# Seven edits to a two-layer transformer kernel: conv border, first pair behind a border, score banks, last head, last weights, constants, first norm

## The chip, the cores and the metric

The kernel runs on one core of a Trainium2 chip, as one launch. The metric is the device time of that launch in microseconds (us). The core has a matrix engine (PE), a vector engine (DVE), an activation engine (ACT) and a general one (POOL), each with its own stream of instructions; SP here only issues DMAs. PE's results go to PSUM, eight banks of 128 x 512 floats; all else lives in SBUF.

## The reference

256 tokens x and 256 context tokens ctx of 1024 features go through two layers. Both layers have the same frame; the middle part is a short convolution in layer 0 and attention (8 query heads of 128, 2 key heads) in layer 1.

```python
def _modulate(t, g, shift, scale):
    return _rms(t, g) * (1 + scale) + shift

def _swiglu(h, w13, w2):
    gte, up = jnp.split(h @ w13, 2, axis=-1)
    return (jax.nn.silu(gte) * up) @ w2
...
    mod = (jax.nn.silu(c) @ mod_w[i] + mod_b[i]).reshape(bsz, 3, 3, 1, D_MODEL)
    lat = lat + 0.5 * mod[:, 0, 2] * _swiglu(_modulate(lat, norm_g[i, 0], mod[:, 0, 0], mod[:, 0, 1]), ffn_w13[i, 0], ffn_w2[i, 0])
    h = _modulate(lat, norm_g[i, 1], mod[:, 1, 0], mod[:, 1, 1])
    y = _short_conv_mixer(h, ...) or _gqa_mixer(h, hc, ...)
    lat = lat + mod[:, 1, 2] * y
    lat = lat + 0.5 * mod[:, 2, 2] * _swiglu(_modulate(lat, norm_g[i, 2], mod[:, 2, 0], mod[:, 2, 1]), ffn_w13[i, 1], ffn_w2[i, 1])
```

The context has the same steps with modulation values of its own (modc) for as long as a later layer reads it. So there are four FFN blocks (0,0), (0,1), (1,0), (1,1), with a mixer between the two of a layer, and a root-mean-square norm over the features ahead of each of the six parts. All is in fp32.

## The kernel before, in words

**Layout.** x holds both token sets as 8 feature tiles (k or m) of 128 partitions by 512 columns, 256 tokens (s = 0) beside 256 context tokens (s = 1). Every fp32 product is three PE matmuls (mm3, L138 to L140): weights and inputs are split into a high part, rounded by an ACT cast (wh, hh, th, bh), and a low part, the rest, by a DVE subtraction (wl, hl, tl, bl); PE adds high by high, high by low, low by high. So each weight tile costs a load (SP), a cast (ACT, L114, L498, L744), a subtraction (DVE, L115, L503, L747) and then PE. Raw weights have two buffers of 2048 columns (wr, load_w L123), the split ones four of 1024 (wh, wl). Half of the FFN's gate/up tiles are done as such plain pairs, the others as block pairs (class Pair), in which sums of weights and of inputs save products: DVE makes the sums (L762 to L769) and the combinations (L804 to L820).

**Order.** In the stretches that the change touches the kernel has a manual schedule: each engine runs its instructions in the order in which the source issues them. Elsewhere a scheduler orders them. SP issues nearly all loads, in order.

**Modulation units.** Beside the first two chunks, the modulation vectors are dot products on DVE: a unit (mod_unit L152) multiplies a 128 x 1024 tile of mod_w (wm, two buffers, loaded by SP at L184) by silu(c) and adds up along the row, 128 x 1024 elements a unit. They are put between other work by tick(n) (L193), which adds n to an account and issues one unit for each whole one in it. PER_PAIR = 0.7 is what a block pair ticks.

**Borders.** Between two parts stands a norm over x that needs the last feature tiles of the part before. class Border (L397) and open_border (L530) write this out. The last two tiles (m = 6, 7) are done in halves: late(s, i) is PE's product for half s of tile 6 + i, fin(i, s) adds the result to x (DVE, L429), square and scaled are ACT's square (L437) and its product with the scale (L412), add adds the square to acc (DVE, L442), sums (PE, L256) adds up acc and the last square over the partitions, root and inv give the reciprocal root, rows (L276) spreads it. PE's order is late(0,0), late(0,1), the first mid tiles of late(1,0), sums(0), the rest of it, rows(0), late(1,1). short is the border behind the conv mixer's output projection, whose products have 8 tiles of depth (nk = KT) in place of 22. There the casts and subtractions of the four weight tiles of the next FFN's first pair (whi, wlo, L498 and L503) stand behind late(0,0), followed by tick(2), which lets DVE do two units ahead of fin(0,0). border_ffn (L825) goes on from there: it does the first gate/up tiles of the FFN in parts, so that PE starts on the tiles of x that are ready, and hands over to the loop over block pairs in ffn (L917). It is used twice, at the FFN blocks (0,1) and (1,0). Its last lines issue post[1].gl() (L906), DVE's subtraction for the second tile's result; the first pair of the loop ticks PER_PAIR at L980.

**The first norm** (L1213 on). Constants come in small loads: ccol (the vectors c), modb, normg, ident (a unit matrix), rowsum on ACT's queue, x in four quarters of two feature tiles each on SP's queue. PE runs 18 matmuls on ones (fill, L1051) in the meantime. The squares of the 8 tiles of x are done by DVE (0, 1, 7) and ACT (2 to 6), added in pairs by DVE (pair_sum, L1125), and summed over features by PE (token_sums, L1129: four matmuls a pair, 128 tokens each, one column of output). ACT's root and DVE's reciprocal follow, then PE spreads the result over the partitions (rb, L1237), and over_rms (L1173) multiplies x by it. Ahead of rb, PE does mod_pe(1, 0), behind it mod_pe(0, 0) (L1142): the first quarter of the scale and of the shift of this norm, as products of silu(c) with rows of mod_w (mr). mod_turn (L1154) turns each from a row to a column, with ACT's copy (row, L1147) ahead of it, and DVE adds bias and one (A, mod). norm_q(0) then makes hh (ACT) and hl (DVE), with which the first gate and up products start (L1202).

**Attention.** use_banks (L1724) gives PSUM to psc (scores, two tiles of two banks), ptp and pav, in that order; at that point the last q projection pq[3] is still in the first banks. weigh (L1655) multiplies the exponentials of a head, two tiles of 128 x 512, by the reciprocal sums on POOL (L1661); PE then turns them (L1672).

**The last projection** (L2013). w_last loads the weights of two output tiles at a time: two pieces of 2048 columns (w2l) and one of 12 x 128 = 1536 (w2m), all three through the two wr buffers.

Of the kernel before, what the change touches and what calls it, by code (L numbers as in the profile page):

```python
# [1 line left out]

# [27 lines left out]
PER_PAIR = 0.7  # L30
WARM = 18
FILL = 5

# [8 lines left out]
def hybrid_kernel(ctx: ExitStack, tc: tile.TileContext, a: dict, out: bass.AP):  # L42
# [29 lines left out]
    def psum(s="ps"):  # L72
        return banks["psm"].tile([P, T2], F32, tag="mm", name=nm(s))
# [3 lines left out]

    def cload(key, shape, eng=None):
        t = const.tile(list(shape), F32, name=key, tag=key)
        (eng or nc.scalar).dma_start(t, a[key])  # L80
        return t


    ccol = cload("ccol", [P, KT, 2])
    x = act.tile([P, KT, T2], F32, name="x", tag="x")
    for q in range(4):
        nc.sync.dma_start(x[:, 2 * q : 2 * q + 2, :], a["xT"][:, 2 * q : 2 * q + 2, :])
    modb = cload("modb", [P, 2, 72])
    normg = cload("normg", [P, 2, 3, KT])
    ident = cload("ident", [P, P])  # L90
    ones = const.tile([P, 1], F32, name="ones", tag="ones")
# [8 lines left out]
    nc.vector.memset(sccol, 0.0)  # L100
    rowsum = cload("rowsum", [P, 2])
    scbc = mp.tile([P, 2, D], F32, name="scbc", tag="scbc", bufs=1)
# [427 lines left out]
    def open_border(bd, v, early=False):  # L530
# [5 lines left out]
        def whi(i):  # L536
            v[i][0].hi(v[i][1])

        def wlo(i):
            v[i][0].lo(v[i][1])  # L540

        ready()
        for s in range(2):
            for k in (4, 5):
                bd.scaled(k, s)
        bd.late(0, 0)
        if short:
            for i in range(2):
                whi(i)
                wlo(i)  # L550
        tick(2)
        bd.fin(0, 0)
# [4 lines left out]
        bd.add(0)  # L557
        bd.fin(1, 0)
        bd.square(1, 0)
        bd.late(1, 0, range(mid))  # L560
# [264 lines left out]
    def border_ffn(l, b, h, bd):  # L825
# [79 lines left out]
        pr.sub(2)  # L905
        post[1].gl()  # L906
        pp.append((psum("pg"), psum("pu")))
        for s in range(2):
# [8 lines left out]
    def ffn(l, b, h, gate, norm, gs=(), ev=1.5, bd=None):  # L917
# [3 lines left out]
        for t in range(2):  # L921
            between = ()
            with tc.manual_schedule(engines=set(QUEUES[:3])) if bd else nullcontext():
# [29 lines left out]
                with nullcontext() if bd else tc.manual_schedule(engines=set(QUEUES[:3])):  # L953
                    for i in range(i1, n):
# [24 lines left out]
                        if prev:  # L979
                            tick(PER_PAIR)  # L980
                            prev.seven()
# [144 lines left out]

    def token_sums(ps, j):
        for i in range(4):
            nc.tensor.matmul(  # L1129
                ps[:, i : i + 1], sqs[2 * j][:, i * P : i * P + P], ones,  # L1130
                start=j == 0 and i == 0, stop=j == 3, skip_group_check=True,
            )
# [80 lines left out]
    with tc.manual_schedule(engines=set(QUEUES)):  # L1213
        for ch, q in ((1, 0), (0, 0)):
            ask_mod(ch, q)
        for i in range(3):
            ask_w(i, 0)
        table(AF.Silu)
        nc.scalar.activation(out=sccol[:, :, :2], in_=ccol, func=AF.Silu)
        table(AF.Sqrt)  # L1220
        nc.vector.tensor_scalar(
            out=sb1, in0=modb[:, 0, KT : 2 * KT], scalar1=1.0, scalar2=None, op0=ALU.add
        )
        ps = psum("ss")
        fill(idle, WARM)
        for k, eng in enumerate((nc.vector, nc.vector) + (nc.scalar,) * 5 + (nc.vector,)):
            square(k, eng)
            if k % 2:
                pair_sum(k // 2)
                token_sums(ps, k // 2)  # L1230
        rs = tp.tile([P, 4], F32, name="rs4", tag="rs4", bufs=1)
        nc.scalar.activation(out=rs, in_=ps[:, :4], func=AF.Sqrt, scale=1.0 / D, bias=eps_t)
        nc.vector.reciprocal(rs, rs)
        mod_pe(1, 0)
        rb = psum("rb")
# [17 lines left out]
        for ch, q in ((1, 1), (0, 1)):  # L1253
            ask_mod(ch, q)
# [51 lines left out]
    for i in range(3):  # L1306
        gs0.append(new_pair("g"))
        w13_post(pps[i], gs0[i], 0, T2)

    convk = cload("convk", [P, 3, KT], nc.sync)  # L1310
    qg = cload("qg", [P, 1], nc.sync)
    kg = cload("kg", [P, 1], nc.sync)


# [340 lines left out]
    def weigh(hd):  # L1655
        e, sm = es[hd]
        r = ap.tile([P, 2], F32, name=nm("r"), tag="r", bufs=3)
        nc.vector.reciprocal(r, sm)
        for qt in range(2):
            c = slice(qt * T2, qt * T2 + T2)  # L1660
            nc.gpsimd.tensor_scalar(  # L1661
                out=e[:, c], in0=e[:, c], scalar1=r[:, qt : qt + 1], scalar2=None, op0=ALU.mult
            )
# [35 lines left out]
    with tc.manual_schedule(engines=set(QUEUES)):  # L1699
# [313 lines left out]
    def w_last(m):  # L2013
        if m // 2 not in box:
            t = m // 2
            box[t] = (
                load_w(a["w2l"][t, 0]), load_w(a["w2l"][t, 1]), load_w(a["w2m"][t], 12 * P)
            )
        o = m % 2
        return lambda k: box[m // 2][o](k * P) if k < 16 else box[m // 2][2]((o * 6 + k - 16) * P)  # L2020

# [8 lines left out]
def _layout(inp):  # L2030
# [52 lines left out]
    d["ident"] = np.eye(P, dtype=np.float32)  # L2083
    d["rowsum"] = (np.arange(P)[:, None] % 32 == np.arange(2)).astype(np.float32)
    return {k: np.ascontiguousarray(v) for k, v in d.items()}

# [18 lines left out]
```

## Time and profile before

| | us |
|---|---|
| median of 3 runs | 1577.05 (1576.33 to 1577.66) |
| profiled execution | 1575.96 |
| its span, first to last instruction | 1573.9 |
| PE busy | 1557.0 |
| DVE busy | 1286.5 |
| ACT busy | 755.2 |
| POOL busy | 34.2 |
| mean granted clock of PE | 0.996 |

How to read it: the profile's page has each engine's busy time, the chain of work that ended last, the costliest groups of instructions and the DMA queues. The trace behind it answers narrower questions: what an engine waited for (a row of the list of waits has the waiting instruction, what released it, us in total, times, longest), when instructions ran (a row of the timeline has start, duration, engine, line, operation, and in brackets the idle time ahead of it with its releaser), and a table by windows of time (for each engine the busy us and, in brackets, the instructions; then the clock that PE was granted, the DMA engines' busy share and GB/s).

### The profile page before, as it was taken

To read this page: it belongs to the slowest core of one execution; us is meant where nothing else is said; L and a number is where in the kernel's file an instruction comes from. 1 tells how busy PE (TensorE), PEld (TensorE's weight loads), DVE (VectorE), ACT (ScalarE), POOL (GpSimd) and SP (SyncE) were. 2 spreads that over 40 slices of the span, in tenths; PEclk is the share of its full clock that TensorE was granted. 3 is DMA by queue.
4 is the path that set the end of the run, shared out by engine and by line. 5 is a ranking of instruction groups with operands and counts; after the bars stand their busy time and mean duration, and the time that the engine had idled before them with its cause. 6 is when DMAs were issued, how large, how long until landed. Compare 5 with 4: busy or idle time off the path is not lost.

```text
span 1573.9 us, 25256 instructions
## 1 busy us (share of the span) xinstructions
PE 1557.0 (99%) x10240; PEld 1422.7 (90%) x10240; DVE 1286.5 (82%) x1905; ACT 755.2 (48%) x1261; POOL 34.2 (2%) x28
## 2 busy tenths in 40 slices
PE   9999999999999989999999999999999999999998
PEld 7789899989888889998999899988999899998887
DVE  5788879996999578996999878997998776776654
ACT  4524245535322365532554475532554465775542
POOL 0000000000000000000000000000000002320000
PEclk9999999999999999999999999999999999999999
DMA  9363633363566412355334523357335632345553
GB/s 360 131 209 130 205 111 131 105 212 132 196 214 199 136 67 99 130 188 162 120 122 146 202 95 121 126 197 240 125 131 194 211 124 87 108 161 193 192 176 136
DMA packets 51747, 248.75 MB, mean 158 GB/s; under 512 B 6704, under 2 KB 9264, under 8 KB 36400
## 3 DMA queue, kind: packets, MB, share of 16 engines
q1 hardware_dynamic: 50912, 246.98, 46.1%
q8 instruction: 80, 1.31, 0.3%
q14 instruction: 35, 0.29, 0.1%
q10 hardware_dynamic: 720, 0.17, 0.0%
HBM read 244.77 MB, written 1.05 MB: 156 GB/s over the span
## 4 chain that ended last, share of the span: by engine, by line
PE 94%; DVE 2%; ACT 1%; DMA 1%; issue 0%; POOL 0%; ACTq 0%; DVEq 0%; POOLq 0%
PE py L138 9%; PE py L140 9%; PE py L139 9%; PE p L138 6%; PE p L140 6%; PE p L139 6%; PE q L140 5%; PE q L138 4%; PE q L139 4%; PE pu L1817 3%; PE pg L1817 3%; PE py L1817 2%; PE pg L522 2%; PE pu L522 2%; PE pg L1202 1%; PE pv L138 1%
## 5 line engine op out<-in xcount | busy, mean ns | idle before, releaser
L114 ACT ACTIVATE wh<-wr 128x1024 fp32r<-128x1024 f32 (+1 forms) x210 | 190.7, 926 | 248.4 <-PE py L139 128.1
L157 DVE CUSTOM_DVE_ANT_0 junk<-wm,scbc,modb 128x1024 bf16<-128x1024 f32 x224 | 286.9, 1281 | 24.6 <-DMA wm<-in_modT 22.7
L115 DVE TENSOR_TENSOR wl<-wr,wh 128x1024 fp32r<-128x1024 f32 (+1 forms) x210 | 220.1, 1060 | 71.8 <-ACT wh L114 29.7
L138 PE MATMUL py<-gh,wh 128*128 128x512 f32 (+1 forms) x594 | 217.8, 367 | 0.0
L139 PE MATMUL py<-gl,wh 128*128 128x512 f32 (+1 forms) x594 | 217.3, 366 | 0.0
L140 PE MATMUL py<-gh,wl 128*128 128x512 f32 (+1 forms) x594 | 217.1, 365 | 0.0
L747 DVE TENSOR_TENSOR wl<-wr,wh 128x1024 fp32r<-128x1024 f32 x156 | 186.1, 1218 | 27.7 <-ACT wh L744 27.7
L744 ACT ACTIVATE wh<-wr 128x1024 fp32r<-128x1024 f32 x156 | 160.5, 1056 | 100.5 <-DVE wr L767 59.0
L140 PEld LDWEIGHTS py<-gh,wl 128*128 128x128 f32 x594 | 112.1, 189 | 17.9
L138 PEld LDWEIGHTS py<-gh,wh 128*128 128x128 f32 x594 | 112.1, 189 | 17.7
L139 PEld LDWEIGHTS py<-gl,wh 128*128 128x128 f32 x594 | 112.1, 189 | 17.6
L140 PE MATMUL p<-th,wl 128*128 128x256 f32 x416 | 117.7, 283 | 0.0
L139 PE MATMUL p<-tl,wh 128*128 128x256 f32 x416 | 117.7, 283 | 0.0
L138 PE MATMUL p<-th,wh 128*128 128x256 f32 x416 | 117.7, 283 | 0.0
L138 PE MATMUL q<-bh,wh 128*128 128x256 f32 x304 | 86.0, 283 | 0.0
L139 PE MATMUL q<-bl,wh 128*128 128x256 f32 x304 | 86.0, 283 | 0.0
L140 PE MATMUL q<-bh,wl 128*128 128x256 f32 x304 | 86.0, 283 | 0.0
L139 PEld LDWEIGHTS p<-tl,wh 128*128 128x128 f32 x416 | 79.8, 192 | 0.2
L138 PEld LDWEIGHTS p<-th,wh 128*128 128x128 f32 x416 | 79.8, 192 | 0.2
L140 PEld LDWEIGHTS p<-th,wl 128*128 128x128 f32 x416 | 79.8, 192 | 0.0
L762 DVE TENSOR_TENSOR wr<-wr 128x1024 f32<-128x1024 f32 x52 | 63.7, 1225 | 1.6
L114 ACT ACTIVATE gh<-gm 128x512 fp32r<-128x512 f32 x60 | 37.8, 631 | 52.1 <-DVE gm L820 47.7
(372 smaller groups left out, 4098.1 us busy)
## 6 DMA issues: line engine op xcount, KB each, us to landing
wr<-in_w SPq DMA_DIRECT2D x85, 1024.0 KB, 4.8
wm<-in_modT SPq DMA_DIRECT2D x128, 512.0 KB, 4.2
wr<-in_w2h SPq DMA_DIRECT2D x48, 704.0 KB, 5.3
mr<-in_mod SPq DMA_DIRECT2D x16, 512.0 KB, 8.5
wr<-in_cw_cx SPq DMA_DIRECT2D x8, 1024.0 KB, 4.8
wr<-in_w2l SPq DMA_DIRECT2D x8, 1024.0 KB, 4.9
wr<-in_cw_b SPq DMA_DIRECT2D x4, 1024.0 KB, 5.2
wr<-in_cw_out SPq DMA_DIRECT2D x4, 1024.0 KB, 5.7
```

What stands on the lines that cost most here:

```text
L114: nc.scalar.activation(out=hi, in_=src, func=AF.Copy)
L115: nc.vector.tensor_tensor(out=lo, in0=src, in1=hi.bitcast(F32), op=ALU.subtract)
L138: nc.tensor.matmul(ps, wh, mh, start=first, stop=False, **kw)
L139: nc.tensor.matmul(ps, wh, ml, start=False, stop=False, **kw)
L140: nc.tensor.matmul(ps, wl, mh, start=False, stop=last, **kw)
L157: nc.vector.tensor_tensor_reduce(out=junk, in0=raw, in1=scbc[:, v, :], scale=1.0, scalar=modb[:, l, col : col + 1], op0=ALU.mult, op1=ALU.add,
L522: nc.tensor.matmul(ps, w[n == 1], hl if n == 2 else hh, start=first and n == 0 and k == ks[0] and (first is True or g == 0), stop=last and ...
L744: nc.scalar.activation(out=self.shaped(g, 0), in_=self.part(g), func=AF.Copy)
L747: nc.vector.tensor_tensor(out=self.shaped(g, 1), in0=self.part(g), in1=self.shaped(g, 0).bitcast(F32), op=ALU.subtract,)
L762: tt(out=by_two(raw[:, :1024]), in0=a21.unsqueeze(1).to_broadcast([P, 2, T2]), in1=by_two(raw)[:, :, :T2], op=ALU.subtract,)
L1202: nc.tensor.matmul(pps[i][j], w[j][n == 1], hl if n == 2 else hh, start=k == 0 and n == 0, stop=k == KT - 1 and n == 2,)
L1817: nc.tensor.matmul(p[:, :n], w(j, k)[part], m(k)[:, :n], start=not part and k == 0, stop=part == 1 and k == nk - 1, skip_group_check=True,)
```

## The change

- **Conv border** (open_border, short alone): the casts and subtractions of the next FFN's first weights are issued ahead of ready(), so ahead of late(0,0) and of the scaled tiles; tick(2) ahead of fin(0,0) becomes tick(1), and a tick(1) stands behind fin(1,0).
- **First pair behind a border**: tick(2) behind post[1].gl(); the first pair of the loop ticks 0 in place of 0.7.
- **Scores**: the banks are given out in the order ptp, pav, psc, so the scores' tiles are in the last four banks.
- **Eighth head**: weigh(7) runs on DVE, the others stay on POOL.
- **Last projection**: w2m comes in two pieces of 768 columns, one for each output tile, through the modulation rows' buffers (wm).
- **Constants**: all eight come in one load of 128 x 364 floats on ACT's queue (convk, qg, kg with them, which SP loaded behind the first norm's loads).
- **x**: the fourth quarter is issued by ACT, the others by SP.
- **First norm**: squares on DVE for 0, 2, 4, on ACT for the others; token sums over pair 0, pair 2, tile 6 alone, pair 4, tile 7 alone; four fills ahead of rb in place of mod_pe(1, 0); behind over_rms the order is product and turn of the scale, product and turn of the shift, with the first weights' casts and subtractions ahead of and behind the last turn; the copy of rb comes behind norm_q(0).

```diff
+CONSTS = (
+    ("ccol", (KT, 2)), ("modb", (2, 72)), ("normg", (2, 3, KT)), ("ident", (P,)),
+    ("rowsum", (2,)), ("convk", (3, KT)), ("qg", (1,)), ("kg", (1,)),
+)
...
+    cst = const.tile([P, sum(sizes)], F32, name="cst", tag="cst")
+    nc.scalar.dma_start(cst, a["cst"])
...
     for q in range(4):
-        nc.sync.dma_start(x[:, 2 * q : 2 * q + 2, :], a["xT"][:, 2 * q : 2 * q + 2, :])
+        eng = nc.scalar if q == 3 else nc.sync
+        eng.dma_start(x[:, 2 * q : 2 * q + 2, :], a["xT"][:, 2 * q : 2 * q + 2, :])
...
+        if short:
+            for i in range(2):
+                whi(i)
+                wlo(i)
         ready()
         for s in range(2):
             for k in (4, 5):
                 bd.scaled(k, s)
         bd.late(0, 0)
-        if short:
-            for i in range(2):
-                whi(i)
-                wlo(i)
-        tick(2)
+        tick(1 if short else 2)
         bd.fin(0, 0)
...
         bd.fin(1, 0)
+        if short:
+            tick(1)
         bd.square(1, 0)
...
         post[1].gl()
+        tick(2)
         pp.append((psum("pg"), psum("pu")))
...
-                            tick(PER_PAIR)
+                            tick(0 if bd and i == i1 else PER_PAIR)
...
-    def token_sums(ps, j):
+    def token_sums(ps, k):
         for i in range(4):
             nc.tensor.matmul(
-                ps[:, i : i + 1], sqs[2 * j][:, i * P : i * P + P], ones,
-                start=j == 0 and i == 0, stop=j == 3, skip_group_check=True,
+                ps[:, i : i + 1], sqs[k][:, i * P : i * P + P], ones,
+                start=k == 0 and i == 0, stop=k == 7, skip_group_check=True,
             )
...
+        ps = psum("ss")
+        fill(idle, WARM)
+        square(0, nc.vector)
+        square(1, nc.scalar)
+        square(2, nc.vector)
+        pair_sum(0)
+        token_sums(ps, 0)
+        square(3, nc.scalar)
+        square(4, nc.vector)
+        pair_sum(1)
+        token_sums(ps, 2)
+        square(5, nc.scalar)
+        square(6, nc.scalar)
+        token_sums(ps, 6)
+        pair_sum(2)
+        token_sums(ps, 4)
+        square(7, nc.scalar)
+        token_sums(ps, 7)
         nc.vector.tensor_scalar(
             out=sb1, in0=modb[:, 0, KT : 2 * KT], scalar1=1.0, scalar2=None, op0=ALU.add
         )
...
-        mod_pe(1, 0)
+        fill(idle, 4)
         rb = psum("rb")
...
         over_rms(0, rb)
-        ris = tp.tile([P, T2], F32, name="ris", tag="gm", bufs=3)
-        nc.scalar.copy(ris, rb)
+        mod_pe(1, 0)
+        mod_turn(1, 0)
         mod_pe(0, 0)
         w_hi(0, 0)
+        mod_turn(0, 0)
         w_lo(0, 0)
-        mod_turn(1, 0)
-        mod_turn(0, 0)
...
         norm_q(0)
+        ris = tp.tile([P, T2], F32, name="ris", tag="gm", bufs=3)
+        nc.scalar.copy(ris, rb)
...
-            nc.gpsimd.tensor_scalar(
+            eng = nc.vector if hd == HEADS - 1 else nc.gpsimd
+            eng.tensor_scalar(
                 out=e[:, c], in0=e[:, c], scalar1=r[:, qt : qt + 1], scalar2=None, op0=ALU.mult
             )
...
-        use_banks(("psc", 2), ("ptp", 2), ("pav", 2))
+        use_banks(("ptp", 2), ("pav", 2), ("psc", 2))
...
-                load_w(a["w2l"][t, 0]), load_w(a["w2l"][t, 1]), load_w(a["w2m"][t], 12 * P)
+            ws = [load_w(a["w2l"][t, j]) for j in range(2)]
+            for j in range(2):
+                raw = mod_raw()[:, : 6 * P]
+                nc.sync.dma_start(raw, a["w2m"][t][:, j * 6 * P : (j + 1) * 6 * P])
+                ws.append(tuple(u[:, : 6 * P] for u in half()))
+                split(*ws[-1], raw)
```

More of the change, by code (lines that the diff above doesn't have):

```diff
@@ L1 @@
 from contextlib import ExitStack, nullcontext
+import math
 import numpy as np
@@ L76, in psmall @@
         return banks["pss"].tile([P, T2], F32, tag="sm", name=nm(s))
[L78 to L84, printed above, removed]
+    sizes = [math.prod(shape) for _, shape in CONSTS]
+    cst = const.tile([P, sum(sizes)], F32, name="cst", tag="cst")
+    nc.scalar.dma_start(cst, a["cst"])
+    ends = np.cumsum(sizes)
+    ccol, modb, normg, ident, rowsum, convk, qg, kg = (
+        cst[:, e - n : e] for e, n in zip(ends, sizes)
+    )
+    ccol = ccol.rearrange("p (k v) -> p k v", v=2)
+    modb = modb.rearrange("p (l c) -> p l c", l=2)
+    normg = normg.rearrange("p (l j k) -> p l j k", l=2, j=3)
+    convk = convk.rearrange("p (n k) -> p n k", n=3)
     x = act.tile([P, KT, T2], F32, name="x", tag="x")
     for q in range(4):
-        nc.sync.dma_start(x[:, 2 * q : 2 * q + 2, :], a["xT"][:, 2 * q : 2 * q + 2, :])
-    modb = cload("modb", [P, 2, 72])
-    normg = cload("normg", [P, 2, 3, KT])
-    ident = cload("ident", [P, P])
+        eng = nc.scalar if q == 3 else nc.sync
+        eng.dma_start(x[:, 2 * q : 2 * q + 2, :], a["xT"][:, 2 * q : 2 * q + 2, :])
     ones = const.tile([P, 1], F32, name="ones", tag="ones")
@@ L100, in hybrid_kernel @@
     nc.vector.memset(sccol, 0.0)
-    rowsum = cload("rowsum", [P, 2])
     scbc = mp.tile([P, 2, D], F32, name="scbc", tag="scbc", bufs=1)
@@ L1223, in hybrid_kernel @@
         )
[L1224 to L1230, printed above, removed]
         rs = tp.tile([P, 4], F32, name="rs4", tag="rs4", bufs=1)
@@ L1308, in hybrid_kernel @@
         w13_post(pps[i], gs0[i], 0, T2)
-    convk = cload("convk", [P, 3, KT], nc.sync)
-    qg = cload("qg", [P, 1], nc.sync)
-    kg = cload("kg", [P, 1], nc.sync)
     hn = Plain()
@@ L2015, in w_last, with at @@
             t = m // 2
-            box[t] = (
-                load_w(a["w2l"][t, 0]), load_w(a["w2l"][t, 1]), load_w(a["w2m"][t], 12 * P)
-            )
-        o = m % 2
-        return lambda k: box[m // 2][o](k * P) if k < 16 else box[m // 2][2]((o * 6 + k - 16) * P)
+            ws = [load_w(a["w2l"][t, j]) for j in range(2)]
[4 more added lines that the diff above has]
+                split(*ws[-1], raw)
+            box[t] = ws
+        o = m % 2
+        ws = box[m // 2]
+        def at(k):
+            if k < 16:
+                return ws[o](k * P)
+            return tuple(u[:, (k - 16) * P : (k - 15) * P] for u in ws[2 + o])
+        return at
     for m in range(KT):
@@ L2084, in _layout @@
     d["rowsum"] = (np.arange(P)[:, None] % 32 == np.arange(2)).astype(np.float32)
+    d["cst"] = np.concatenate(
+        [np.asarray(d.pop(key)).reshape(P, -1) for key, _ in CONSTS], axis=1
+    )
     return {k: np.ascontiguousarray(v) for k, v in d.items()}
```

## The prediction, made before the changed kernel ran

> **What bounds the kernel now.** The first view is the profile's page: the span, the engines' shares, and the chain that ended last.
>
> ```profile
> span 1573.9 us, 25256 instructions
> ...
> PE 1557.0 (99%) x10240; PEld 1422.7 (90%) x10240; DVE 1286.5 (82%) x1905; ACT 755.2 (48%) x1261; POOL 34.2 (2%) x28
> ...
> PE 94%; DVE 2%; ACT 1%; DMA 1%; issue 0%; POOL 0%; ACTq 0%; DVEq 0%; POOLq 0%
> ```
>
> PE is busy for 1557.0 of 1573.9 us and is 94% of the chain. The change touches hardly any matmul of the stream, so it can win only where PE stands still or runs at a lower clock, and it can lose only there too. The second view is therefore the list of PE's waits.
>
> ```profile
> PE ss L256 <- DVE acc L442: 3.9, 1, 3.9
> PE ss L1129 <- DVE sq L1125: 1.7, 1, 1.7
> PE psc L138 <- ACT kn L1447: 1.3, 1, 1.3
> PE pt L1672 <- POOL e L1661: 1.2, 2, 0.9
> ...
> PE p L140 <- DVE wl L747: 0.9, 2, 0.5
> PE pg L1202 <- ACT hh L1186: 0.7, 1, 0.7
> ...
> PE py L1817 <- ACT wh L114: 0.4, 2, 0.2
> ...
> PE ss L256 <- ACT sq L437: 0.3, 1, 0.3
> ```
>
> Each row is one place: the border after the conv mixer (L256), the first norm (L1129, L1202), the first scores (L138 with psc), the turned heads (L1672), the first FFN pair behind a border (L140), the last projection (L1817). The third view is the table by windows, for the granted clock (the column after POOL).
>
> ```profile
> 4.00:11.00 7.00, 5.33 (x47) 5.14 (x46) 4.27 (x8) 5.37 (x10) 0.00 (x0) 1.00 1.03 365
> 11.04:17.86 6.82, 6.82 (x43) 4.93 (x46) 1.17 (x4) 0.64 (x2) 0.00 (x0) 0.50 1.03 358
> 560.58:567.41 6.83, 5.41 (x24) 5.33 (x25) 2.03 (x6) 2.59 (x7) 0.00 (x0) 0.50 0.42 158
> 612.00:618.00 6.00, 5.49 (x44) 5.08 (x43) 5.93 (x9) 3.32 (x5) 0.00 (x0) 1.00 0.27 90
> 1526.00:1562.00 36.00, 35.50 (x195) 29.68 (x195) 16.36 (x20) 14.29 (x18) 0.00 (x0) 1.00 0.54 180
> ```
>
> Twice, for 6.83 us, PE has half its clock: at the first norm and at the conv border, each time soon after PE stood idle. The list of waits doesn't show that price.
>
> **The conv border (6.5 us less).**
>
> ```profile
> 550.35 0.88 DVE L594 SCALAR_TENSOR_TENSOR x<-py,mod,x 128x256 f32<-128x256 f32 x2 [3.11 <-PE py L140]
> 554.41 1.99 ACT L498 ACTIVATE wh<-wr 128x1024 fp32r<-128x1024 f32 x2
> 555.49 2.36 DVE L503 TENSOR_TENSOR wl<-wr,wh 128x1024 fp32r<-128x1024 f32 x2 [2.82 <-ACT wh L498]
> 557.77 1.28 DVE L157 CUSTOM_DVE_ANT_0 junk<-wm,scbc,modb 128x1024 bf16<-128x1024 f32 x1
> ...
> 559.09 1.28 DVE L157 CUSTOM_DVE_ANT_0 junk<-wm,scbc,modb 128x1024 bf16<-128x1024 f32 x1
> ...
> 560.30 0.48 DVE L429 SCALAR_TENSOR_TENSOR x<-py,mod,x 128x256 f32<-128x256 f32 x1
> 561.26 0.42 DVE L442 TENSOR_TENSOR acc<-acc,sq 128x256 f32<-128x256 f32 x1 [0.48 <-ACT sq L437]
> ...
> 561.74 0.58 PE L256 MATMUL ss<-ones,acc 128*128 128x1 f32 x2 [3.89 <-DVE acc L442]
> ```
>
> PE ran dry at 561.74 - 3.89 = 557.85. Ahead of the addition that it waited for, DVE had two weight subtractions (2.36) and two modulation units (1.28 each). The change puts the casts and subtractions before the tile that closes at 550.35, and one unit behind the second x. ACT and DVE have idle time there (2.82 before the subtractions). If one subtraction still falls behind the x of 550.35, DVE goes 550.35 + 0.88 + 1.18 + 0.69 (its addition) + 1.28 = 554.4, and the chain from x to the sums (560.30 to 561.74, 1.44) ends at 555.8, two us before PE asks. The second wait (0.3) is for the other half's square: its x can start once PE has closed the second block, 1.8 us before the sums (15 matmuls of 0.12), and takes 0.48 and a square of 0.42, so it goes too. The unit that stands behind that x ends about 558, before the reciprocal is due. With no idle time I expect no drop of the clock: 5.41 us of PE work at 0.50 is 2.7 at full clock, less what the engines beside it need, 2.4. Sum 3.9 + 0.3 + 2.4 = 6.6, taken as 6.5; ends 3.5 (something else is late there) and 7.
>
> **The first FFN pair behind a border, twice (1.3 us less).**
>
> ```profile
> 605.98 1.23 DVE L747 TENSOR_TENSOR wl<-wr,wh 128x1024 fp32r<-128x1024 f32 x1 [3.18 <-ACT wh L744]
> 612.32 1.22 DVE L747 TENSOR_TENSOR wl<-wr,wh 128x1024 fp32r<-128x1024 f32 x1
> ```
>
> The unit that stood ahead of the subtraction at 612.32 goes; two are done instead in the 3.18 us in which DVE was idle before 605.98 (2.7 of them). The subtraction comes 1.3 earlier, and the list's 0.9 goes; the window 612 to 618 has 0.51 of PE idle, so 1.0 for two places, and with the slower pace behind a wait I take 1.3; ends 0.5 and 2.1. The units' rows were loaded long before; their order only moves forward, and their number stays.
>
> **Scores (0.4 less).**
>
> ```profile
> 1323.23 0.16 DVE L1658 RECIPROCAL r<-sm 128x2 f32<-128x2 f32 x1
> 1323.58 3.10 POOL L1661 TENSOR_SCALAR e<-e,r 128x512 f32<-128x512 f32 x2 [1323.15 <-DVE r L1658]
> ```
>
> With other banks the first scores no longer wait 1.3 us for the scaled q. But the first turn of a head waits for POOL's product (1.55 each, first done at 1325.1), which waits for DVE's r; that row has no idle time ahead of it, so DVE comes there from work that the banks don't speed up. Most of the 1.3 comes back as a wait there. I take 0.4; ends 0 and 1.3.
>
> **Eighth head (1.0 less).**
>
> ```profile
> 1352.16 3.10 POOL L1661 TENSOR_SCALAR e<-e,r 128x512 f32<-128x512 f32 x2 [0.60 <-DVE r L1658]
> L1375 DVE TENSOR_SCALAR d<-u,convk x8: 477/481/487, 405.1 to 515.5; 128x512 f32<-128x512 f32 x8
> ```
>
> On DVE the two products take 0.96 in place of 3.10, so they are done about 2 us sooner; PE's wait of 0.9 goes with what stands beside it. DVE's subtraction for head six comes up to 0.9 later, which may cost PE some tenths. 1.0; ends 0.3 and 1.3.
>
> **Last projection (1.0 less).**
>
> ```profile
> ACT wh L114 <- DMA wr<-in_w2m: 10.8, 3, 4.9
> ```
>
> The third piece of the weights of a block takes buffers of the modulation rows, free by then, so its load no longer stands in line behind two others; ACT waited 10.8 for it. PE felt only 0.4 in waits, 0.50 idle in the window 1526 to 1562. With the pace behind these waits I take 1.0; ends 0.3 and 2.
>
> **The start (4.0 us more).**
>
> ```profile
> 8.51 4.79 PE L1129 MATMUL ss<-ones,sq 128*128 128x1 f32 x32 [1.67 <-DVE sq L1125]
> ...
> 15.09 2.08 PE L1237 MATMUL rb<-ident,rs 128*128 128x128 f32 x8
> 17.09 1.42 PE L1142 MATMUL pr<-mr,sccol 128*32 128x256 f32 x16
> 18.45 0.61 PE L1154 MATMUL pr<-rowsum,row 128*128 128x2 f32 x4
> ...
> 22.07 0.50 PE L1202 MATMUL pg<-hh,wh 128*128 128x512 f32 x1 [0.75 <-ACT hh L1186]
> ```
>
> ```profile
> 9.88 0.69 DVE L1119 TENSOR_TENSOR sq<-x 128x512 f32<-128x512 f32 x1 [0.23 <-DMA x<-in_xT]
> ...
> 19.06 0.38 ACT L1147 COPY row<-pr 128x256 f32<-128x256 f32 x1
> ...
> 20.92 2.08 ACT L1186 ACTIVATE hh<-hr,mod,A 128x256 fp32r<-128x256 f32 x4 [0.86 <-DVE mod L1159]
> ```
>
> From 22.07 on PE runs on, so the time at which the first product starts is what this part wins or loses. The last quarter of x lands at 9.88, and a quarter (512 KB) takes 1.44 us at the 365 GB/s of the window 4 to 11; the DMA share there is full (1.03). Quarters landed about 5.6, 7.0, 8.4 and 9.9. Taken on two queues, the second and the fourth share the rate and land together about 8.4, the third at 9.9. [...]
>
> DVE then squares quarter two until 9.1 and adds until 9.8: the sums begin at 9.8, not 8.51. They are five groups of 8 records, not four: at full clock a group is 0.9 (0.112 a record), at half 1.7 (0.213); 23 records from 8.51 to 11.04 and 9 more to the end make up the row's 4.79. PE has stood idle longer than before, so I take it that the clock drops at 11.04 again. Before, one group ran after that; now four do: 9.9 to 10.8, then 11.3 to 18.1, where before the sums ended at 13.3. Better landings by half a us and a group already under way make it 17.2.
>
> Then, before: root, reciprocal, the first modulation product in their shade, rb at 15.09 to 17.17, 4.9 to the first product. Now: root and reciprocal 0.65 under 4 fills (0.9 to 1.7), rb 1.0 to 2.0, and behind it one after the other product 1.42, copy 0.38 and waits, turn 0.61, product 1.42, copy, turn, B, hh, which is 2 x (1.42 + 0.5 + 0.61) + 1.5 = 6.5 to the first product. With the sums done at 17.2 and full clock from 17.86: fills to 18.1, rb to 19.1, first product at 25.7: 3.6 later. With half clock on: 27.6, 5.5 later; with 18.1 and half clock, 28.3, 6.2 later. With no drop of the clock at all the sums end at 14.4 and the product starts at 22.8, 0.7 later. I take 4.0, near the row's own 6.83 us of half clock; ends 0.5 and 6.5. Loads of small constants that go from SP spare a few tenths of issue that nothing waits for.
>
> **Sum.** 6.5 + 1.3 + 0.4 + 1.0 + 1.0 = 10.2 less and 4.0 more: 6.2 less. The profiled execution took 1575.96 (its span and 2.1 around it), which gives 1569.8; the median of the runs is 1577.05, 1.1 above it, so I say 1570.8. All ends together: 4.6 to 13.7 of gain against 0.5 to 6.5 of loss.
>
> **The rivals.** *The start costs nothing.* If the squares come early enough for the sums to run before the clock drops, the start loses 0.5 and the whole gain stands: 1577.05 - 9.7 = 1567.4, or 1566 if the small gains are at their upper ends. For it: DVE's first square no longer waits for another load. Against it: 40 records for 32 and a third quarter of x that lands last. Chance 0.20.
>
> *The border doesn't yield.* If the early casts wait for the buffers that the last output tiles still read, ACT holds the square behind them and PE is late as before; then 1570.8 + 6.5 = 1577.3, no change. Against it: 2.82 us of DVE idle and free buffers by 550. Chance 0.10.
>
> *Slower: the half clock at the start does not end.* Sums of one column and products of 32 columns may not count as work for the clock. In the trace, PE is busy 6.82 of 6.82 us from 11.04 to 17.86, with just such work in much of it, and has half its clock all that time. Each further 3.41 us of half clock in the stream costs 1.7. The gain of 6.2 is gone after 3.6 of them, at about 30 us, and it is slower by over 0.2% from six on, at about 38 us; by seven it is 1570.8 + 11.9 = 1582.7. [...] Chance 0.06.
>
> **How the numbers follow.** The forecast has 0.64 (1567.5 to 1574). Runs of this kernel differ by 1.3, so about 0.2%, 3.2 us, is what can be told from no change. Faster by more (below 1573.9): forecast and first rival, 0.84. Same: 0.10. Slower: 0.06. The range goes from the first rival's lower end to the forecast with 6.5 lost at the start: 1565 to 1574.
>
> **What would show it.** Right: no row "ss L256 <- DVE acc" in PE's waits and no clock of 0.50 after 20 us; first product at 24 to 28; POOL's e as what PE waits for at the first turn; no DMA in ACT's waits for w2m. Wrong: a first product at or before 23, sums that run at full clock, a wait of several us moved to the rows or the first gate product behind the border.

## The result and the profile after

The changed kernel takes 1567.72 us (median of 4 runs, 1567.13 to 1569.16) against 1577.05: 9.3 us less, ratio 0.9942 (95% interval 0.9925 to 0.996). The forecast was 1570.8 in a range of 1565 to 1574. Its profiled execution took 1567.13. Lines of helpers moved down by 7 to 18: L256 is now L263, L442 is L449, L1129 is L1139, L1672 is L1690.

The profile's page of the changed kernel:

```profile
span 1565.4 us, 25277 instructions
...
PE 1555.1 (99%) x10256; PEld 1423.8 (91%) x10256; DVE 1286.6 (82%) x1906; ACT 755.3 (48%) x1261; POOL 31.1 (2%) x26
...
PE 93%; DVE 3%; DMA 3%; issue 1%; ACT 0%; POOL 0%; SPq 0%; DVEq 0%; POOLq 0%
```

The list of PE's waits:

```profile
PE ss L1139 <- DVE sq L1135: 2.1, 2, 1.6
PE pt L1690 <- POOL e L1679: 1.4, 2, 1.1
...
PE pr L1164 <- ACT row L1157: 1.0, 2, 0.5
PE pt L1690 <- DVE ptl L1556: 0.3, 1, 0.3
PE pg L1212 <- ACT hh L1196: 0.2, 1, 0.2
PE p L147 <- DVE wl L756: 0.2, 1, 0.2
```

The waits for acc (3.9), for the last square (0.3), for kn (1.3), for wh in the last projection (0.4) are gone, and that for wl fell from 0.9 to 0.2. What stays is the first norm, where the wait for the squares is 2.1 in place of 1.7. New is a wait of 1.1 for POOL at the first head's turn (in the row with 1.4), where the list of before had its 0.9 at the eighth head. The border in the timeline, DVE's rows and PE's first sums:

```profile
553.35 0.87 DVE L603 SCALAR_TENSOR_TENSOR x<-py,mod,x 128x256 f32<-128x256 f32 x2 [0.63 <-PE py L147]
554.21 1.23 DVE L510 TENSOR_TENSOR wl<-wr,wh 128x1024 fp32r<-128x1024 f32 x1
555.35 0.69 DVE L254 TENSOR_TENSOR acc<-acc,sq 128x512 f32<-128x512 f32 x1
555.95 1.28 DVE L164 CUSTOM_DVE_ANT_0 junk<-wm,scbc,cst 128x1024 bf16<-128x1024 f32 x1
...
558.21 0.42 DVE L449 TENSOR_TENSOR acc<-acc,sq 128x256 f32<-128x256 f32 x1 [0.58 <-ACT sq L444]
```

```profile
560.70 0.28 PE L263 MATMUL ss<-ones,acc 128*128 128x1 f32 x2
```

acc is done at 558.63, PE asks at 560.70: 2.1 us to spare, and PE's row carries no idle time. The first norm, PE's rows:

```profile
9.31 1.05 PE L1139 MATMUL ss<-ones,sq 128*128 128x1 f32 x8 [1.58 <-DVE sq L1135]
10.92 5.20 PE L1139 MATMUL ss<-ones,sq 128*128 128x1 f32 x32 [0.56 <-DVE sq L1135]
15.98 2.06 PE L1061 MATMUL idle<-sones 128*128 128x128 f32 x8
17.83 1.91 PE L1258 MATMUL rb<-cst,rs 128*128 128x128 f32 x8
...
25.41 0.50 PE L1212 MATMUL pg<-hh,wh 128*128 128x512 f32 x1 [0.23 <-ACT hh L1196]
```

The sums end at 16.1 in place of 13.3, and the first product starts at 25.41 in place of 22.07, 3.3 later. This is the part that loses. The table by windows shows why the sums took so long:

```profile
9.50:12.92 3.42, 2.86 (x26) 2.77 (x25) 1.98 (x4) 1.67 (x3) 0.00 (x0) 1.00 1.02 398
12.92:16.33 3.41, 3.41 (x17) 3.41 (x17) 0.00 (x0) 0.17 (x1) 0.00 (x0) 0.50 1.07 384
16.33:19.74 3.41, 3.41 (x20) 3.19 (x23) 0.18 (x1) 0.09 (x1) 0.00 (x0) 0.50 1.03 411
```

Half clock lasted from 12.92 to 19.74, as long as before (6.82), but 1.9 later.

### The profile page after: what moved, and what is told of

It reads as the page before. It is cut to its first block, busy times and chain, and to the rows that moved or that the text cites. A ratio compares the mean times of both kernels' runs of the same rounds, so it can differ in the third digit from the quotient of the medians.

```text
span 1565.4 us, 25277 instructions
## 1 busy us (share of the span) xinstructions
PE 1555.1 (99%) x10256; PEld 1423.8 (91%) x10256; DVE 1286.6 (82%) x1906; ACT 755.3 (48%) x1261; POOL 31.1 (2%) x26
## 4 chain that ended last, share of the span: by engine, by line
PE 93%; DVE 3%; DMA 3%; issue 1%; ACT 0%; POOL 0%; SPq 0%; DVEq 0%; POOLq 0%
PE py L145 8%; PE py L147 8%; PE py L146 8%; PE p L145 6%; PE p L147 6%; PE p L146 6%; PE q L147 5%; PE q L145 5%; PE q L146 5%; PE py L1835 4%; PE pu L1835 3%; PE pg L1835 3%; PE pg L529 2%; PE pu L529 2%; DMA wm<-in_modT 2%; PE pg L1212 1%
## 5 line engine op out<-in xcount | busy, mean ns | idle before, releaser
L164 DVE CUSTOM_DVE_ANT_0 junk<-wm,scbc,cst 128x1024 bf16<-128x1024 f32 x224 | 286.8, 1280 | 30.4 <-DMA wm<-in_modT 28.6
L121 ACT ACTIVATE wh<-wr 128x1024 fp32r<-128x1024 f32 (+1 forms) x202 | 184.3, 929 | 243.1 <-PE py L146 123.9
L122 DVE TENSOR_TENSOR wl<-wr,wh 128x1024 fp32r<-128x1024 f32 (+1 forms) x202 | 212.8, 1064 | 57.5 <-ACT wh L121 26.6
```

Source lines behind the costliest of these rows:

```text
L121: nc.scalar.activation(out=hi, in_=src, func=AF.Copy)
L122: nc.vector.tensor_tensor(out=lo, in0=src, in1=hi.bitcast(F32), op=ALU.subtract)
L164: nc.vector.tensor_tensor_reduce(out=junk, in0=raw, in1=scbc[:, v, :], scale=1.0, scalar=modb[:, l, col : col + 1], op0=ALU.mult, op1=ALU.add,
```

## Experiments

Medians are of the runs of each kernel. Ratios are to the kernel before, timed beside each group of experiments, where its median was 1575.2 to 1576.9. In the diffs + is the experiment, - what it starts from.

**The start, four kernels.** s1_old_start takes the whole start of before:

```diff
-    nc.scalar.dma_start(cst, a["cst"])
+    ccol = cload("ccol", [P, KT, 2])
...
-        eng = nc.scalar if q == 3 else nc.sync
...
-        square(0, nc.vector)
...
-        token_sums(ps, 7)
+        for k, eng in enumerate((nc.vector, nc.vector) + (nc.scalar,) * 5 + (nc.vector,)):
...
-        fill(idle, 4)
+        mod_pe(1, 0)
```

> The changed kernel with the whole start of before (separate constant loads, x on one queue, old order of the first norm); all other edits stay. In the profile of the changed kernel the first product starts at 25.41 us, before at 22.07. My theory, that the start loses what its first product is later by: first product at 22.1, some 3.3 us faster than the changed kernel, about 1564.4. Rival, that the later start is made good again further on: about 1567.7, no change.

1562.89 us (1562.79 to 1563.46), ratio 0.9916 (0.9902 to 0.9929); 4.8 faster than the changed kernel by the medians, 4.1 by the ratios. Its first product starts 4.1 sooner, and runs at half clock until 23.11:

```profile
21.34 0.79 PE L1211 MATMUL pg<-hh,wh 128*128 128x512 f32 x1
```

The start's loss is real, and it isn't made good further on. This version beats both kernels.

s2_old_order keeps the new loads alone, s3_old_loads the new order alone:

```diff
-        square(0, nc.vector)
...
-        token_sums(ps, 7)
+        for k, eng in enumerate((nc.vector, nc.vector) + (nc.scalar,) * 5 + (nc.vector,)):
...
```

> New loads (one load of constants, a quarter of x on ACT's queue), old order of the first norm. If the order is what costs: sums end near 13.5 and the first product starts at 22 to 23, about 1564.5 to 1565. If the loads are what costs (the second quarter of x lands at 7.9 in place of 7): first product at 24 or later, 1567 or more.

1564.76 (1564.44 to 1565.1), ratio 0.9928.

```diff
-    cst = const.tile([P, sum(sizes)], F32, name="cst", tag="cst")
+    ccol = cload("ccol", [P, KT, 2])
...
```

> Old loads, new order of the first norm. If the order is what costs: first product at 24.5 to 26, about 1567.5. If the loads are: first product near 22 to 23, 1564.5 to 1565.

1567.16 (1565.61 to 1568.64), ratio 0.9941. The starts of the first product, one row from the timeline of each (s2, then s3):

```profile
23.39 0.50 PE L1212 MATMUL pg<-hh,wh 128*128 128x512 f32 x1 [0.74 <-ACT hh L1196]
```

```profile
24.58 0.50 PE L1211 MATMUL pg<-hh,wh 128*128 128x512 f32 x1 [0.22 <-ACT hh L1195]
```

The order costs most: 4.3 us with the old loads (1567.16 - 1562.89), 3.0 with the new. The loads cost 1.9 with the old order and 0.6, within the scatter, with the new. The profiled executions say the same, with other sizes and less scatter. All four have 6.83 us of half clock at the start, and PE reaches the sums of its first border at 376.3 (s1), 378.1 (s2), 379.2 (s3) and 380.0 (the changed kernel). So the order costs 2.8 with the old loads and 1.9 with the new, the loads 1.7 and 0.8. Neither cause holds alone.

s4_mod_first puts back what stands behind the sums:

```diff
-        fill(idle, 4)
+        mod_pe(1, 0)
         rb = psum("rb")
...
-        mod_pe(1, 0)
-        mod_turn(1, 0)
         mod_pe(0, 0)
         w_hi(0, 0)
-        mod_turn(0, 0)
         w_lo(0, 0)
+        mod_turn(1, 0)
+        mod_turn(0, 0)
```

> The changed kernel, but behind the sums the order of before: the first modulation product stands ahead of the spreading of the reciprocal in place of the four fills, and the second product stands ahead of both turns. The sums keep their new order. If the row of products, copies and turns behind the spreading costs what I summed (6.5 against 4.9), this is 0.8 to 1.5 us faster than the changed kernel, 1566.2 to 1566.9, and the rest of the 3.3 stays with the sums. Rival, that the sums cost nothing of their own: all 3.3 back, 1564.4.

1567.03 (1566.35 to 1568.24), ratio 0.9942: 0.7 faster by the medians, nothing by the ratios. The profiled execution had a longer stretch of half clock (10.24 us, the changed kernel's had 6.82), which may be why so little came of it. In its windows of 3.41 us:

```profile
6.91:10.33 3.42, 2.27 (x19) 1.99 (x17) 2.42 (x4) 2.51 (x7) 0.00 (x0) 1.00 0.98 373
10.33:13.74 3.41, 3.18 (x15) 3.19 (x16) 0.86 (x3) 0.55 (x2) 0.00 (x0) 0.50 0.98 386
13.74:17.15 3.41, 3.41 (x17) 3.41 (x18) 0.00 (x0) 0.00 (x0) 0.00 (x0) 0.50 1.08 384
17.15:20.57 3.42, 3.42 (x24) 2.13 (x24) 0.18 (x1) 0.64 (x2) 0.00 (x0) 0.50 1.03 411
```

Here the clock dropped at 10.33 and stayed low for three windows. From 13.74 to 17.15 PE ran nothing but token sums, 3.41 of 3.41 us, and the clock didn't rise; it rose after the window with the modulation product and rb.

**The conv border, three kernels.** b1_old_border:

```diff
-        if short:
-            for i in range(2):
-                whi(i)
-                wlo(i)
         ready()
...
         bd.late(0, 0)
-        tick(1 if short else 2)
+        if short:
+            for i in range(2):
+                whi(i)
+                wlo(i)
+        tick(2)
...
-        if short:
-            tick(1)
```

> The changed kernel with the old conv border. My theory (a wait of 3.9 and 0.3 us and a drop of the clock that it brings): 6.5 to 7 us slower than the changed kernel, 1574.5, with a stretch of half clock behind the border. Rival, that the clock drops only by chance of its phase: 4.2 us slower, 1572, and no half clock there.

1574.49 (1573.78 to 1576.18, 11 runs), ratio 0.999 (0.9981 to 0.9998): 6.8 slower than the changed kernel. Its waits, and the window behind the border:

```profile
PE ss L263 <- DVE acc L449: 3.9, 1, 3.9
...
PE ss L263 <- ACT sq L444: 0.5, 1, 0.5
```

```profile
567.58:570.99 3.41, 3.41 (x17) 3.41 (x17) 0.65 (x2) 0.55 (x2) 0.00 (x0) 0.50 0.11 46
```

Wait and half clock are back. In this execution the half clock lasted 3.41 us, in that of before 6.83. The idle time was about the same, its place in the windows of 3.41 us differed: before had 2.7 us of it in the window that ended with the drop and 1.4 in the next one, b1 had 1.9 in one window, without a drop, and 2.5 in the next, which ended with the drop.

b3_casts_only leaves both units where they were:

```diff
-        tick(1 if short else 2)
+        tick(2)
...
-        if short:
-            tick(1)
```

> The changed kernel with the casts and subtractions early, but both units ahead of the first x again. By the sum of the prediction the margin is two us and a unit is 1.3, so PE still doesn't wait: 1567.7, no difference. Rival, that the units are what matters: a wait of 1 us or more at the sums, 1569 or more.

1568.04 (1567.48 to 1570.16), ratio 0.9948: no difference that can be told. PE waits for nothing at the border, with 0.8 us to spare (acc ends at 563.53):

```profile
563.11 0.42 DVE L449 TENSOR_TENSOR acc<-acc,sq 128x256 f32<-128x256 f32 x1 [0.48 <-ACT sq L444]
```

```profile
564.35 0.28 PE L263 MATMUL ss<-ones,acc 128*128 128x1 f32 x2
```

b4_ticks_only leaves the casts late and moves the unit alone:

```diff
-        if short:
-            for i in range(2):
-                whi(i)
-                wlo(i)
         ready()
...
         bd.late(0, 0)
+        if short:
+            for i in range(2):
+                whi(i)
+                wlo(i)
         tick(1 if short else 2)
```

> The changed kernel with the casts late again, but only one unit ahead of the first x. PE then waits some 2.6 us in place of 3.9. If the drop of the clock hangs on how much of one 3.4 us window is idle: either no drop (2.6 to 3 slower than the changed kernel, 1570.5) or the whole drop (5 slower, 1573).

1573.51 (1571.24 to 1575.8, 11 runs), ratio 0.998 (0.9971 to 0.9989): 5.8 slower than the changed kernel by the medians. The wait is as worked out, and the profiled execution has the whole drop:

```profile
PE ss L263 <- DVE acc L449: 2.6, 1, 2.6
```

```profile
564.83:571.65 6.82, 5.99 (x27) 5.91 (x28) 3.62 (x7) 2.35 (x7) 0.00 (x0) 0.50 0.53 202
```

The runs spread over 4.6 us, more than those of any other kernel here. The mean granted clock of each run goes with it: 0.997 in the two fastest (1571.2 and 1571.6), 0.993 in the four slowest (1574.2 to 1575.8). Where in the others the clock was low isn't known, as only one execution has a profile, and that one had 13.65 us of half clock at the start too (the changed kernel 6.83). The sizes by PE's rows below leave the start out. So the early casts bring the gain; the split of the ticks adds margin only.

**The other parts, against s1_old_start (1562.89).** p1_old_pairs:

```diff
         post[1].gl()
-        tick(2)
...
-                            tick(0 if bd and i == i1 else PER_PAIR)
+                            tick(PER_PAIR)
```

> The changed kernel with the old start (1562.89) and the old ticks around the first block pair. In the profiles before and after, what PE loses at the two borders in and behind the first pair goes from 0.62 + 0.21 twice, with small losses behind them, to 0.1 or less: some 2 us slower, 1564.9. If only what the list of waits shows counts (0.9): 1563.8.

1564.51 (1564.03 to 1566.38), ratio 0.9933: 1.6 slower by the medians, 2.7 by the ratios. The row of before is back:

```profile
PE p L146 <- DVE wl L755: 0.9, 2, 0.5
```

p2_old_last:

```diff
-                raw = mod_raw()[:, : 6 * P]
...
+                load_w(a["w2l"][t, 0]), load_w(a["w2l"][t, 1]), load_w(a["w2m"][t], 12 * P)
```

> The changed kernel with the old start (1562.89) and the old loads of the last projection's weights. By the prediction 1.0 slower, 1563.9; by the three groups of losses of before (0.7, 0.5, 0.7 with the slower pace behind each wait) 1.9 slower, 1564.8. If the wait of ACT for the load counted in full (10.8): over 1570.

1565.2 (1563.91 to 1566.18), ratio 0.9936: 2.3 slower by the medians, 3.1 by the ratios. In the list:

```profile
PE py L1825 <- ACT wh L120: 0.9, 3, 0.4
```

PE starts later three times, as before; the wait grew from 0.4 to 0.9 here, and with the slower pace behind each wait the 1.9 of the second expectation is nearest. In the trace of before the product at 1528.26 starts 0.62 behind the one ahead of it and the next one 0.34 behind it, where the others start 0.23 apart: 0.50 lost at a listed wait of 0.24.

p3_old_heads:

```diff
-        use_banks(("ptp", 2), ("pav", 2), ("psc", 2))
+        use_banks(("psc", 2), ("ptp", 2), ("pav", 2))
...
-            eng = nc.vector if hd == HEADS - 1 else nc.gpsimd
-            eng.tensor_scalar(
+            nc.gpsimd.tensor_scalar(
```

> The changed kernel with the old start (1562.89), the old order of the banks and the eighth head's products on POOL again. My theory: 0.3 for the banks, since the wait only moved to the first turn, and 0.8 for the eighth head, 1564.0; PE's waits show the scores' 1.3 in place of the first turn's 1.0, and 0.9 at the eighth head. Rival, that the banks gained the whole 1.3: 1565.0, and the first turn's wait stays.

1564.72 (1563.53 to 1565.44), ratio 0.9932: 1.8 slower by the medians, 2.5 by the ratios. PE's waits in p3, then in s1:

```profile
PE psc L144 <- ACT kn L1454: 1.3, 1, 1.3
PE pt L1679 <- POOL e L1668: 1.2, 2, 0.9
```

```profile
PE pt L1680 <- POOL e L1669: 1.3, 2, 1.0
...
PE pt L1680 <- DVE ptl L1546: 0.3, 1, 0.3
```

2.5 us of waits fall to 1.6, not to 0.3: of the scores' 1.3, most comes back at the first turn, where PE waits 1.0 for POOL. The time is nearer to the rival's 1565.0 than to my 1564.0, but the rival, that the banks gained the whole 1.3, is refuted by the rows, as the first turn's wait doesn't stay but moves. Counted from the sums ahead of attention, p3 starts its scores 1.5 later than s1, its first turn only 0.4 later and the next border's sums 1.2 later. So the banks brought 0.4 and the eighth head 0.8.

v3_first_head takes that wait away too, on top of s1:

```diff
-            eng = nc.vector if hd == HEADS - 1 else nc.gpsimd
+            eng = nc.vector if hd in (0, HEADS - 1) else nc.gpsimd
```

> The changed kernel with the old start (1562.89) and the first head's products on DVE too, as the eighth's. PE waits 1.0 there for POOL; DVE has the first half ready 1.1 sooner. If the product is the only thing late: 1.0 faster, 1561.9. Rival, that DVE, which has no pause there, gives it back in what it does later (subtractions for v and q, the next maxima): no difference, 1562.9, with a new wait of PE for DVE.

1562.4 (1561.41 to 1563.23), ratio 0.991 (0.9896 to 0.9923). PE's waits for POOL fall to 0.3:

```profile
PE pt L1680 <- POOL e L1669: 0.3, 1, 0.3
PE pt L1680 <- DVE ptl L1546: 0.3, 1, 0.3
```

The wait went, and no other row grew. The medians say 0.5, within the scatter of the runs. PE's rows settle it: between the sums ahead of attention and those behind it v3 takes 118.0, s1 118.9, so 0.9 was won.

**The sizes by PE's rows.** The start's clock moves the medians of runs by more than some of these parts are worth. The sums at the borders (the rows ss<-ones,acc of PE's timeline) divide each profiled execution into stretches, and only the first holds the start. Times are us of PE from sums to sums:

| stretch | before | changed | the edit undone |
|---|---|---|---|
| start of the span to the border behind the first FFN | 377.0 | 380.0 | s1 376.3 |
| over the conv border and the first pair, to the border behind the second FFN | 536.5 | 528.7 | b1 535.0, b4 534.6, b3 528.7, p1 529.6 |
| over the next first pair, to the border behind the third FFN | 351.1 | 350.1 | p1 350.7 |
| attention, to the border behind it | 120.1 | 118.9 | p3 120.1 |
| last FFN, to the end of the span | 189.3 | 187.7 | p2 189.8 |

Kernels in which a stretch has the same edits agree there within 0.2 us, with one exception: in the third stretch s1, s2, s3, s4, b1, b3 and b4 take 349.4 to 349.5, and the changed kernel 0.7 more (its 0.2 of waits for wl lie there), for a cause that stays open. Against 349.4, p1 loses 1.3 there, and 0.8 in the second stretch. So the border is worth 6.3 and the early casts all of it (b3 loses nothing, b4 5.8 of the 6.3), the two pairs 2.2, scores and eighth head 1.2, the last projection 2.2, and the start costs 3.7.

The first stretch holds the scatter. In the six profiled executions with the start of before (before, s1, p1, p2, p3, v3) it takes 375.8 to 377.0, with 3.4 to 6.8 us of half clock. In the four with the new one (the changed kernel, b1, b3, b4) it takes 380.0 to 383.6, with 6.8 to 17.1 us. So the new start also brought longer stretches of half clock in three of its four executions.

**The clock.** v2_fills, on top of s1:

```diff
                 token_sums(ps, k // 2)
+                fill(idle, 2)
```

> The changed kernel with the old start (1562.89) and two more fills behind each group of token sums (16 records of 128 columns among 32 of one column). In the runs so far every window of 3.41 us that held little but sums ended in half clock, also where PE was busy all through it. If what counts is how much of a window is work of many columns and a third of it is enough: no half clock before 18 us, and about 1562.5. If it is not enough: the same stretch of half clock and the fills' 1.3 us on top, 1564.2.

1563.52 (1562.11 to 1566.4), ratio 0.9925. The profiled execution, the slowest of the five at 1566.4:

```profile
11.10:14.52 3.42, 3.42 (x19) 3.42 (x18) 0.63 (x1) 0.00 (x0) 0.00 (x0) 0.50 1.02 406
14.52:17.93 3.41, 3.41 (x26) 2.47 (x25) 0.18 (x1) 0.26 (x1) 0.00 (x0) 0.50 0.92 290
17.93:21.34 3.41, 3.41 (x24) 2.18 (x20) 0.74 (x2) 0.37 (x1) 0.00 (x0) 0.50 1.02 386
```

With a third of wide records among the sums the clock was at half in this execution too, for 10.24 us. But in the two fastest runs (1562.1 and 1562.2) the mean granted clock is 1.000, which no run of another kernel here reaches and which leaves less than 1.6 us at half clock, where the shortest stretch in a profile here is 3.41. So with two fills a group the drop came in the profiled execution and, by the granted clock, not in two of the five runs. Whether the fills kept it away there isn't shown, as those runs have no profile; they are 0.7 to 0.8 faster than s1's median.

## Why the prediction held, point by point

**That only PE's gaps count: right.** PE is 99% busy in both kernels, and each edit is worth what it takes from PE's gaps, not what it takes from an engine: in the last projection ACT waited 10.8 us for the load, and PE's gain was some 2.

**The conv border (6.5): right in cause and size.** Without it 6.8 are lost by the medians and 6.3 by PE's rows (b1). The step that I argued from two rows, that the half clock behind the border belongs to the idle time and goes with it, is borne out: with the idle time the half clock is back (b1 has 3.41 us of it behind waits of 3.9 and 0.5, b4 6.82 behind 2.6 and 0.3), without it there is none (the changed kernel, b3). The margin of two us was measured as 2.1. What I didn't see is that the casts alone are enough (b3).

**Block pairs (1.3): right in cause, too small.** 1.6 by the medians, 2.2 by PE's rows, just above my upper end of 2.1; PE's 0.9 of waits and the slower pace behind them. In the trace of before the product at 613.60 starts 0.74 behind the one ahead of it and the next one 0.22 behind it, where the others start 0.12 apart: 0.72 lost at a listed wait of 0.46.

**Scores and eighth head (0.4 and 1.0): right.** 1.8 together by the medians, but 0.4 and 0.8 by PE's rows. The wait at the first turn came where it was forecast.

**Last projection (1.0): right in cause, mis-sized.** 2.3 by the medians and 2.2 by PE's rows (p2), 1.7 between before and the changed kernel. I went by PE's idle time in the window (0.50) and doubled it; a wait cost more than its listed time (0.50 for 0.24 at 1528.26).

**The start (4.0 more): right in sign, and in size partly by luck.** The product started 3.3 later, and undoing the start gives 4.1 to 4.8 by the runs, 3.7 by PE's rows. The sums ended at 16.1, not at 17.2 to 18.1, since the clock dropped at 12.92 and not at 11.04. My step "the clock drops at 11.04 again" took a moment of one execution for a property of the kernel: the first drop came at 12.92 in the changed kernel, at 10.33 in s4 and at 10.05 in b3. In b3's execution, with the same start as the changed kernel's, the product started at 28.70, 6.6 later than before and beyond my upper end of 6.5. That the changed kernel's 25.41 came so near to the 25.7 of my sum is luck. And the loads, which I counted as half a quarter's delay within the new order, cost 1.9 by themselves with the old one (s2). The serial chain behind rb, which I priced at 6.5 from rb's end to the first product against 4.9, took 5.7 (19.74 to 25.41), all at full clock.

**The rivals.** That the start costs nothing, and that the border doesn't yield, are refuted by s1 and b1. The third, that the half clock doesn't end, happened in part, and not with the new start alone: s1 has a second stretch from 19.69 to 23.11. In b3's profiled execution, the slowest of its runs at 1570.16, two stretches of half clock stood ahead of 31 us:

```profile
10.05:23.70 13.65, 13.18 (x69) 11.60 (x68) 3.33 (x7) 1.83 (x4) 0.00 (x0) 0.50 1.03 398
27.12:30.53 3.41, 3.41 (x14) 3.05 (x13) 3.31 (x10) 3.26 (x8) 0.00 (x0) 0.50 1.04 413
```

Its price came out smaller than the rival needed: with 10.24 us more of half clock than the changed kernel, this execution reached the first border 3.7 later, 1.2 for each 3.41 us and not the 1.7, half of 3.41, that I had estimated, and the run is 2.1 above the median of its kernel. The stretches of half clock in the profiles here last 3.41, 6.83, 10.24 and 13.65 us. What the rival supposed of one-column sums fits one window: s4's from 13.74 to 17.15 held nothing else, was busy 3.41 of 3.41 us, and the clock was 0.50 in it and in the window behind it.

That the second and the fourth quarter of x would share one rate was my estimate from the full DMA share of before. From 4 to 11 us all loads together moved 393 GB/s at a share of 1.01 in the changed kernel, against 365 at 1.03 before. In the changed kernel's timeline DVE's squares of the second and the third quarter of x start as these land:

```profile
7.96 0.69 DVE L1129 TENSOR_TENSOR sq<-x 128x512 f32<-128x512 f32 x1 [1.74 <-DMA x<-in_xT]
...
9.57 0.69 DVE L1129 TENSOR_TENSOR sq<-x 128x512 f32<-128x512 f32 x1 [0.32 <-DMA x<-in_xT]
```

The quarter that landed last came at 9.57 on two queues and at 9.88 on one, and the second one at 7.96, later than the 7.0 that I had worked out for one queue.

**The sum.** 9.3 less by the medians against 6.2 forecast. The spans of the two profiled executions differ by 8.5, and PE's rows divide it: the start 3.0 more, the conv border with the first pair 7.7 less, the second pair's stretch 1.0 less, attention 1.1 less, the last projection 1.7 less. Against the terms of my sum the start lost 1.0 less than 4.0, the border and both pairs won 0.9 more than 7.8, the last projection 0.7 more than 1.0, scores and eighth head 0.3 less than 1.4. Three of the four errors go the same way, so they added up and didn't cancel. Two numbers of the range were summed wrongly: the first rival with the small gains at their upper ends (0.8, 0.9, 0.3 and 1.0 more) is 1564.4, not 1566, and the forecast with 6.5 lost at the start is 1573.3. The range as stated, 1565 to 1574, is about that wide all the same.

## What to carry to other kernels

Where one engine bounds the kernel, price each edit by that engine's gaps, and add what a gap does to its clock afterwards: at the border 4.2 us of waiting cost 6.3 to 6.8. Work moved into idle time ahead of the gap (here the casts) was worth the whole gap; moving the unit as well added nothing that can be told. Where the start alone moves a kernel's time by several us, size an edit elsewhere by the starts of the same instructions in the traces, not by medians. Test the parts of a bundled change one at a time: here the edits at the start cost 4 us that the others hid, and the kernel without them (1562.9, with the first head on DVE 1562.4) beats both.

## What the runs showed of the hardware that was not expected

- In the profiles of before and of the changed kernel the clock changed whole steps of 3.41 us after its first rise: that came at 4.21 before, with drops at 11.04 and 560.58 (2 and 163 steps of 3.413), and at 6.09 in the changed kernel, with its drop at 12.92 (2 steps). The rise is read from the fills' starts, 0.21 apart ahead of it and 0.11 behind it. The half clock at the start lasted 6.82 us in the changed kernel, 10.24 in s4 and 13.65 in b3, and runs of one kernel differ by up to 4.6 us (b4, where the slower ones have the lower mean granted clock, 0.993 against 0.997).
- In a window full of one-column sums the granted clock was 0.50, and in the next one too, though PE was busy 3.41 of 3.41 us (s4, 13.74 to 17.15). With a third of 128-column work among the sums it was 0.50 for 10.24 us in v2's profiled execution, while two other runs of v2 have a mean granted clock of 1.000.
- Around a wait of 2.6 us at the border the clock was 0.50 for 6.82 us (b4), as long as around 3.9 us before (6.83). PE had stood idle for 2.0 us of the window of 3.41 us ahead of the drop; behind a window with 1.9 us idle there was none in b1.
